# A score row's negated maximum is scaled on ScalarE instead of VectorE

## The chip, the cores and the metric

The kernel runs on one core of a Trainium2 chip. A core has five engines with a queue of instructions each: TensorE (PE in the profile; its weight loads are PEld), VectorE (DVE), ScalarE (ACT), GpSimd (POOL) and SyncE (SP), which here issues the DMAs. An engine takes its instructions in the order of its queue; engines wait for each other through semaphores. The metric is the time on the device in microseconds, lower is better.

## The reference

One layer of an encoder is applied to two groups ("prompt" and "sample") of 1024 tokens with 1024 channels. What matters here are its two attention branches, which read the same normalised input:

```python
qa = rms_norm(qa.reshape(B, S, HQ_A, HEAD_DIM), qn_a)
...
s = jnp.einsum('bqgrd,bkgd->bgrqk', qblk, k).astype(jnp.float32) * scale
p = jax.nn.softmax(s, axis=-1).astype(v.dtype)
return jnp.einsum('bgrqk,bkgd->bqgrd', p, v)
...
p = jax.nn.softmax(s, axis=-1)
pd = (p[:, :, 0] - lam * p[:, :, 1]).astype(v.dtype)
```

Branch A has 8 query heads on 2 key heads of 64 dimensions. Branch B has 4 heads with two softmax maps each, of which the second is subtracted with a learned weight. Queries are normalised by their root mean square before the scores are taken. Around the branches stand one wide input projection, gates with a sigmoid or SiLU, two branch projections, an output projection and a residual add.

## The kernel before

Tokens lie in tiles of 128 rows. Each projection splits its float32 operands into a rounded high part and a low part and adds three products; weights come from memory in four pieces, are rounded on ScalarE (L195), and their low part is taken on GpSimd (L197). The projections of queries, keys and values are L574 (128x256), those of the gates L764 (128x512). TensorE transposes the normalised rows (L637), and ScalarE and VectorE write the two parts of the transposed queries and keys (L639, L640).

A **score unit** (softmax_unit) is one tile of 128 queries against all 1024 keys for one head or map: 256 of them in all, 128 per branch. Four matmuls (L798, L799) fill a PSUM tile s of 1024 columns, of which there are two in turn. VectorE takes the negated maximum of each row into the one-column tile m (L800). The query's inverse root mean square, rs, was not multiplied into the query; it is multiplied into m (L801) and given to the exponential as its scale (L802), so that ScalarE computes exp(rs * s + rs * (-max)) and the row sum in one instruction. m comes from a pool of six buffers, the result p from one of four.

VectorE then transposes p in blocks of 32x32 (L843; in branch B it first subtracts the second map, L842), four DMAs lay the blocks out for TensorE (L852), and a **value unit** multiplies with the values (L866 in branch A, L883 in branch B). The score units of the next query tiles run ahead of these value units.

The code emits attention steps and projection steps interleaved by weights (weave), with a higher priority for attention. A scheduler then sets the order of every engine's queue from a simulated timeline, so that a change of one instruction can move others on all queues. Projections that are ready fill TensorE between score and value units.

Of the kernel before, what the change touches and what calls it, by code (L numbers as in the profile page):

```python
# [14 lines left out]
AF = mybir.ActivationFunctionType  # L15
ALU = mybir.AluOpType
# [73 lines left out]
def kernel(ctx: ExitStack, tc: tile.TileContext, t: dict):  # L90
    nc = tc.nc
# [17 lines left out]
    def nm(s):  # L109
        uid[0] += 1  # L110
        return f"{s}_{uid[0]}"

    def sbank():
        return ps_s.tile([P, 1024], F32, tag="s", name=nm("s"))
# [677 lines left out]
    def softmax_unit(q, sw, k, pt, su, rs):  # L792

        m = tiny.tile([P, 1], F32, tag="m", name=nm("m"))
        s = sbank()
        for n in range(2):
            sl = slice(n * 512, (n + 1) * 512)
            nc.tensor.matmul(s[:, sl], q, k[:, sl], start=True, stop=False)  # L798
            nc.tensor.matmul(s[:, sl], sw, k[:, sl], start=False, stop=True)  # L799
        nc.vector.tensor_reduce(out=m, in_=s, axis=AX.X, op=ALU.max, negate=True)  # L800
        nc.vector.tensor_tensor(out=m, in0=m, in1=rs, op=ALU.mult)  # L801
        nc.scalar.activation(  # L802
            pt.rearrange("p (j c a) -> p j c a", j=4, c=8), s.rearrange("p (c a j) -> p j c a", c=8, j=4),
            AF.Exp, bias=m, scale=rs, accum_out=su,
        )

    def scores(u, i):

        pairs = "h" not in u
        t, m = (i % 2, i // 2) if pairs else (i // 2, i % 2)  # L810
        qt = u["pr"] * 2 + t
        if "sw" not in u:
            u["sw"] = swapped(u)
        pt = ptile()
        if pairs:
            su = u["su"][:, m, qt : qt + 1]
        else:
            su = u["su"][:, qt : qt + 1] if m == 0 else tiny.tile([P, 1], F32, tag="su", name=nm("su"))
        softmax_unit(u["q"][m][:, qt * P : (qt + 1) * P], u["sw"][:, m, t * P : (t + 1) * P], u["k"][m], pt, su, u["rs"][m][:, qt])
        if pairs:  # L820
            u[m, t] = [pt]
            return m, t
        if m == 0:
            u[t] = [pt]
        else:
            f = tiny.tile([P, 1], F32, tag="r", name=nm("r"))
            nc.vector.reciprocal(f, su)
            nc.gpsimd.tensor_scalar(
                out=f, in0=f, scalar1=u["su"][:, qt : qt + 1], scalar2=nlam, op0=ALU.mult, op1=ALU.mult
            )  # L830
            u[t] += [pt, f]
        return (0, t) if m else None
# [559 lines left out]
```

## Time and profile before

| | us |
|---|---|
| timed runs, median of 3 | 1882.31 |
| timed runs, lowest and highest | 1879.48, 1884.93 |
| profiled execution, its span from first to last instruction | 1880.0 |
| median less span | 2.3 |
| TensorE's granted clock, mean share of full speed | 0.995 |

The profiled execution is known by its span; what lies around the span is taken as the 2.3 us to the median. In the profile, a group's line has the line of the kernel, the engine, the operation, output and inputs by name, shapes and count, then the busy time in us, the mean of one in ns, and the engine's idle time before the group with what ended it. In the list of waits, a line has who waited, for whom, the sum in us, how often, and the longest. The windows' lines have start and end, and then the busy time of TensorE, of its weight loads, of VectorE, ScalarE and GpSimd.

### The profile page before, as it was taken

Reading aid. Unit: us, or ns where it says so; the run is one execution under the profiler, and the core shown is the slowest. Engines: PE = TensorE matmul, PEld = TensorE weight load, DVE = VectorE, ACT = ScalarE, POOL = GpSimd, SP = SyncE. Lnnn points to the kernel's source line nnn. Section 1 sums busy time; section 2 is a strip of 40 time slices with the busy share of each in tenths; the row PEclk is TensorE's granted clock in tenths of the full one; section 3 lists DMA queues with packets and bytes.
Section 4 is the critical chain, followed back from the end, with each engine's and each line's share of the span. In section 5 each row is a group of like instructions: output and inputs, shape, how many; then the busy total and the mean of one; then the engine's idle time right before and its main releaser. Section 6 shows DMA issues by size and latency. Waiting matters only on the chain.

```text
span 1880.0 us, 29891 instructions
## 1 busy us (share of the span) xinstructions
PE 1836.5 (98%) x10398; PEld 1550.6 (82%) x10398; DVE 1222.3 (65%) x2016; ACT 780.1 (41%) x1544; POOL 607.1 (32%) x888
## 2 busy tenths in 40 slices
PE   6999999999999999999999999999999999999999
PEld 3798877888899977888889888888888898888887
DVE  5777766454777777347466687666357766663795
ACT  4544434344554444313223445344345545442241
POOL 1243311433454451221233333014354635222100
PEclk8999999999999999999999999999999999999999
DMA  9135776555444567754631567666524343675442
GB/s 324 57 94 160 208 198 178 146 168 163 111 127 113 162 188 219 244 152 140 206 131 52 156 177 204 189 186 188 158 68 141 106 129 103 176 247 173 128 127 92
DMA packets 283895, 295.46 MB, mean 157 GB/s; under 512 B 41952, under 2 KB 236640, under 8 KB 283744
## 3 DMA queue, kind: packets, MB, share of 16 engines
q1 hardware_dynamic: 283744, 293.54, 53.1%
q8 instruction: 83, 1.36, 0.3%
q14 instruction: 68, 0.56, 0.1%
HBM read 133.98 MB, written 42.01 MB: 94 GB/s over the span
## 4 chain that ended last, share of the span: by engine, by line
PE 68%; DMA 4%; issue 3%; DVE 3%; SPq 3%; POOL 2%; ACT 1%; ACTq 0%; DVEq 0%; POOLq 0%
PE f L764 15%; PE f L574 15%; PE f L1038 7%; PE a L883 5%; PE s L798 4%; PE s L799 4%; PE a L866 4%; PE s L1038 3%; PE f L1073 3%; PE s L1073 2%; PE f L1145 2%; SPq L852 1%; DMA q<-p 1%; DMA st<-in_w_in_dram 1%; PE s L1145 1%
## 5 line engine op out<-in xcount | busy, mean ns | idle before, releaser
L764 PE MATMUL f<-u,w 128*128 128x512 f32 x2232 | 565.1, 395 | 0.8 <-POOL w L197 0.4
L574 PE MATMUL f<-w,u 128*128 128x256 f32 x3456 | 478.6, 287 | 0.9 <-POOL w L197 0.4
L764 PEld LDWEIGHTS f<-u,w 128*128 128x128 f32 x2232 | 409.8, 188 | 82.6 <-POOL w L197 1.1
L574 PEld LDWEIGHTS f<-w,u 128*128 128x128 f32 x3456 | 452.3, 193 | 22.3 <-issue 3.5
L800 DVE TENSOR_REDUCE m<-s 128x1 f32<-128x1024 f32 x256 | 309.6, 1218 | 98.8 <-PE s L799 97.4
L197 POOL TENSOR_TENSOR w<-st,w 128x512 fp32r<-128x512 f32 x160 | 213.2, 1350 | 357.9 <-ACT w L195 342.1
L843 DVE STREAM_TRANSPOSE p<-p 128x1024 f32<-128x1024 f32 x192 | 237.7, 1243 | 87.9 <-ACT p L802 73.5
L802 ACT ACTIVATE p<-s,m,u 128x1024 f32<-128x1024 f32 x128 | 153.9, 1204 | 160.0 <-issue 57.8
L802 ACT ACTIVATE p<-s,m,rsB 128x1024 f32<-128x1024 f32 x128 | 154.0, 1204 | 118.7 <-DVE m L801 97.1
L799 PE MATMUL s<-u,sw 128*128 128x512 f32 x512 | 201.1, 397 | 0.0
L195 ACT ACTIVATE w<-st 128x512 fp32r<-128x512 f32 x184 | 108.2, 626 | 112.4 <-DMA st<-in_w_in_dram 97.5
L1038 PE MATMUL f<-u,w 128*128 128x512 f32 x552 | 131.0, 392 | 0.0
L883 PE MATMUL a<-q,u 128*128 128x256 f32 x512 | 126.5, 380 | 4.0 <-DMA q<-p 3.7
L597 POOL TENSOR_TENSOR rsB<-ss,nhalf 128x4 f32<-128x4 f32 x64 | 68.1, 1064 | 184.7 <-DVE ss L596 160.6
L866 PE MATMUL a<-q,u 128*64 128x256 f32 x1024 | 117.7, 382 | 3.6 <-DMA q<-p 2.9
L1038 PEld LDWEIGHTS f<-u,w 128*128 128x128 f32 x552 | 103.0, 188 | 21.1
L798 PE MATMUL s<-u 128*128 128x512 f32 x256 | 107.9, 425 | 2.7 <-ACT p L802 2.7
L799 PEld LDWEIGHTS s<-u,sw 128*128 128x128 f32 x512 | 96.5, 189 | 16.4
L640 DVE TENSOR_TENSOR u<-f,u 64x256 fp32r<-64x256 f32 (+1 forms) x198 | 81.3, 411 | 42.9 <-ACT u L639 37.5
L883 PEld LDWEIGHTS a<-q,u 128*128 128x128 f32 x512 | 93.5, 190 | 18.8 <-issue 3.4
L772 ACT ACTIVATE ev<-f 128x512 f32<-128x512 f32 x93 | 55.3, 595 | 128.5 <-PE f L764 72.5
L866 PEld LDWEIGHTS a<-q,u 128*64 128x64 f32 x1024 | 73.8, 137 | 40.3 <-issue 7.2
(221 smaller groups left out, 2174.6 us busy)
## 6 DMA issues: line engine op xcount, KB each, us to landing
q<-p SPq DMA_DIRECT2D x768, 128.0 KB, 2.6
st<-in_w_in_dram SPq DMA_DIRECT2D x132, 256.0 KB, 3.3
zd<-ev SPq DMA_DIRECT2D x96, 256.0 KB, 2.7
sw<-u SPq DMA_DIRECT2D x256, 64.0 KB, 2.0
u<-in_w_ada_dram SPq DMA_DIRECT2D x8, 1024.0 KB, 11.7
oo<-zd SPq DMA_DIRECT2D x64, 128.0 KB, 2.4
od<-oo SPq DMA_DIRECT2D x64, 128.0 KB, 2.4
st<-in_w_in_dram SPq DMA_DIRECT2D x64, 128.0 KB, 2.7
```

The source lines that it names most:

```text
L195: hi = nc.scalar.activation(wh, st, AF.Copy)
L197: lo = e.tensor_tensor(out=wl, in0=st, in1=wh.bitcast(F32), op=ALU.subtract)
L574: ins = nc.tensor.matmul(ps, lt[c][:, sl], w[:, c, wi, :], start=(k == 0), stop=(k == 23))
L764: ins = nc.tensor.matmul(ps, w[:, c, wi, e * P : (e + 1) * P], rt[c], start=(k == 0), stop=(k == 23),)
L798: nc.tensor.matmul(s[:, sl], q, k[:, sl], start=True, stop=False)
L799: nc.tensor.matmul(s[:, sl], sw, k[:, sl], start=False, stop=True)
L800: nc.vector.tensor_reduce(out=m, in_=s, axis=AX.X, op=ALU.max, negate=True)
L802: nc.scalar.activation(pt.rearrange("p (j c a) -> p j c a", j=4, c=8), s.rearrange("p (c a j) -> p j c a", c=8, j=4), AF.Exp, bias=m, scal ...
L843: nc.vector.transpose(pt, pt)
L866: lambda k=k, m=m: nc.tensor.matmul(acc[(LO, HI)[m]], u["v"][:, k], pT[m][:, k], start=(k == 0), stop=(k == 7))
L883: nc.tensor.matmul(acc, u["v"][:, k], pT[:, k], start=(k == 0), stop=(k == 7))
L1038: nc.tensor.matmul(ps, w[:, c, wi, d * P : (d + 1) * P], o[:, oi, :], start=(k == 0), stop=(k == 11))
```

## The change

The multiplication of m by rs leaves VectorE's queue. ScalarE does it as a copy of one column with rs as its scale, ahead of the exponential that reads m.

```diff
         nc.vector.tensor_reduce(out=m, in_=s, axis=AX.X, op=ALU.max, negate=True)
-        nc.vector.tensor_tensor(out=m, in0=m, in1=rs, op=ALU.mult)
+        nc.scalar.activation(m, m, AF.Copy, scale=rs)
         nc.scalar.activation(
```

The scheduler then orders all queues anew. Three places show it. The numbers in names are those of the tiles; equal names are the same tile in both kernels.

VectorE's queue before, where the second group's branch A begins its second half (near 1160 us in the trace), for the score tiles s_11509 and s_11546:

```order
L800 TENSOR_REDUCE m_11508<-s_11509 128x1
L800 TENSOR_REDUCE m_11545<-s_11546 128x1
L801 TENSOR_TENSOR m_11508<-m_11508,u_9478 128x1
L801 TENSOR_TENSOR m_11545<-m_11545,u_9478 128x1
L774 SCALAR_TENSOR_TENSOR ev_11719<-ev_11719,f_11616 128x512
L843 STREAM_TRANSPOSE p_11507<-p_11507 128x1024
```

The first multiply stands behind the second reduce. VectorE's queue after, for the same two units:

```order
L800 TENSOR_REDUCE m_11508<-s_11509 128x1
L843 STREAM_TRANSPOSE p_11492<-p_11492 128x1024
L843 STREAM_TRANSPOSE p_11507<-p_11507 128x1024
L774 SCALAR_TENSOR_TENSOR ev_11529<-ev_11529,f_11397 128x512
L872 TENSOR_TENSOR oo_11407<-a_11409,oo_11407 128x4x2x32
L800 TENSOR_REDUCE m_11545<-s_11546 128x1
```

The multiplies are gone, and the second reduce has moved behind two transposes.

TensorE's queue before, behind the score tile s_11788 in the same stretch:

```order
L799 MATMUL s_11788<-u_9477,sw_11593 128x512
L764 MATMUL f_11750<-u_9123,w_11733 128x512
L764 MATMUL f_11750<-u_9121,w_11733 128x512 x2
L764 MATMUL f_11750<-u_9123,w_11733 128x512
L764 MATMUL f_11750<-u_9121,w_11733 128x512 x2
L764 MATMUL f_11750<-u_9123,w_11733 128x512
```

In all, 33 matmuls of L764 and L574 stand there before the next score tile, s_11882. TensorE's queue after, at the same tile:

```order
L799 MATMUL s_11788<-u_9477,sw_11593 128x512
L574 MATMUL f_11703<-w_11685,u_9122 128x256
L574 MATMUL f_11703<-w_11685,u_9120 128x256 x2
L574 MATMUL f_11703<-w_11685,u_9122 128x256
L798 MATMUL s_11882<-u_9477,u_10432 128x512
L799 MATMUL s_11882<-u_9477,sw_11593 128x512
L798 MATMUL s_11882<-u_9477,u_10432 128x512
L799 MATMUL s_11882<-u_9477,sw_11593 128x512
L798 MATMUL s_11901<-u_9477,u_10433 128x512
```

Four matmuls of L574 are left between the first two score tiles; s_11901 and s_11932 follow s_11882 with nothing between, then a value unit, then s_11969 and s_12061.

ScalarE's queue before, for three of these score tiles:

```order
L802 ACTIVATE p_11786,suA_138<-s_11788,m_11787,u_9478 128x1024
L772 ACTIVATE ev_11846<-f_11750 128x512
L802 ACTIVATE p_11880,suA_138<-s_11882,m_11881,u_9478 128x1024
L749 ACTIVATE u_11702<-f_11870 128x256
L802 ACTIVATE p_11899,suA_138<-s_11901,m_11900,u_9478 128x1024
```

ScalarE's queue after, from the exponential of s_11788 to the roundings of weights that come behind that of s_11932:

```order
L802 ACTIVATE p_11786,suA_138<-s_11788,m_11787,u_9478 128x1024
L801 ACTIVATE m_11881<-m_11881,u_9478 128x1
L772 ACTIVATE ev_11719<-f_11616 128x512
L802 ACTIVATE p_11880,suA_138<-s_11882,m_11881,u_9478 128x1024
L801 ACTIVATE m_11900<-m_11900,u_9478 128x1
L802 ACTIVATE p_11899,suA_138<-s_11901,m_11900,u_9478 128x1024
L801 ACTIVATE m_11931<-m_11931,u_9478 128x1
L802 ACTIVATE p_11930,suA_138<-s_11932,m_11931,u_9478 128x1024
L195 ACTIVATE w_11685<-st_11694 128x2x256
L195 ACTIVATE w_11685<-st_11698 128x2x256
L195 ACTIVATE w_11733<-st_11734 128x2x256
```

The copies (L801) are new. A tanh (L772) now stands between the copy of m_11881 and its exponential, and pieces of the weights w_11685 and w_11733, which were rounded further ahead before, come behind the exponential of s_11932.

## The prediction

> **What bounds the kernel now.** I read the page's head first, then what TensorE waited for.
>
> ```profile
> span 1880.0 us, 29891 instructions
> PE 1836.5 (98%) x10398; PEld 1550.6 (82%) x10398; DVE 1222.3 (65%) x2016; ACT 780.1 (41%) x1544; POOL 607.1 (32%) x888
> ```
>
> TensorE is busy in 98% of the span, VectorE in 65%, ScalarE in 41%. The change moves work between two engines that have room, so it can touch the end only where TensorE stands still: 1880.0 - 1836.5 = 43.5 us. The windows of 47 us place that idle time.
>
> ```profile
> 0.00:47.00 47.00, 29.47 (x154) 18.08 (x155) 25.59 (x46) 20.65 (x36) 8.87 (x13) 0.85 0.90 324
> 47.00:94.00 47.00, 42.42 (x260) 36.78 (x259) 37.48 (x111) 24.46 (x67) 13.51 (x15) 0.96 0.18 57
> ```
>
> The first number behind the length is TensorE's busy time: 17.5 + 4.6 = 22.1 us of the idle time lie in the first two windows, where no score row exists yet. The rest, 21.4 us, is all that this profile shows to be won. TensorE's waits name its parts.
>
> ```profile
> PE s L798 <- ACT p L802: 4.2, 6, 1.2
> PE a L883 <- DMA q<-p: 3.7, 4, 1.5
> PE f L637 <- POOL row L626: 3.4, 2, 3.2
> PE a L866 <- DMA q<-p: 2.9, 4, 1.3
> PE a L866 <- issue: 0.8, 1, 0.8
> PE a L883 <- issue: 0.3, 1, 0.3
> ```
>
> Two of these hang on the chain that the change edits. A score unit (L798, L799) waits until the exponential (L802) has emptied one of two PSUM buffers: 4.2 us. A value unit (L866, L883) waits for the transposed exponentials to land: 3.7 + 2.9 + 0.8 + 0.3 = 7.7 us. So at most 11.9 us hang on the length of the chain reduce, multiply, exponential, transpose, DMA.
>
> **The multiplication itself.** These groups, with shapes kept apart, carry the prices.
>
> ```profile
> L800 DVE TENSOR_REDUCE m<-s 128x1 f32<-128x1024 f32 x256 | 309.6, 1218 | 98.8 <-PE s L799 97.4
> L801 DVE TENSOR_TENSOR m<-m,u 128x1 f32<-128x1 f32 x128 | 28.2, 226 | 2.7
> L801 DVE TENSOR_TENSOR m<-m,rsB 128x1 f32<-128x1 f32 x128 | 26.6, 215 | 1.9
> L802 ACT ACTIVATE p<-s,m,rsB 128x1024 f32<-128x1024 f32 x128 | 154.0, 1204 | 118.7 <-DVE m L801 97.1 <-issue 11.7 <-DMA q<-p 3.3
> L384 ACT ACTIVATE cT<-cT 128x16 f32<-128x16 f32 x1 | 0.2, 216 | 0.0
> L487 ACT ACTIVATE lam<-lam 128x2 f32<-128x2 f32 x1 | 0.2, 203 | 1.0 <-DVE lam L486 1.0
> L639 ACT ACTIVATE u<-f 64x256 fp32r<-64x256 f32 x182 | 68.3, 375 | 71.2 <-DVE u L640 47.7 <-PE f L637 21.9
> ```
>
> Removed from VectorE: 128 x 226 + 128 x 215 ns = 28.2 + 26.6 = 54.8 us. Added to ScalarE: 256 one-column copies. No row shows one; the nearest are activations on 2 and 16 columns, 203 and 216 ns, and a copy of 256 columns at 375 ns stands above. I take 0.21 us, from the nearest: 256 x 0.21 = 54 us (41 at the 0.159 of VectorE's median multiply, below, and 96 at 0.375 are the ends). ScalarE goes from 780 to some 834 us, 44% of the span, VectorE to 1167. Neither becomes the bound. The multiply's own line gives shortest, median and longest, in ns, which the means hide:
>
> ```profile
> L801 DVE TENSOR_TENSOR m<-m,u x128: 116/159/1260, 130.4 to 1337.5; 128x1 f32<-128x1 f32 x128
> L801 DVE TENSOR_TENSOR m<-m,rsB x128: 118/159/1308, 458.3 to 1682.0; 128x1 f32<-128x1 f32 x128
> ```
>
> The copy issues no DMA and sits at the place in ScalarE's queue where the exponential waited already, so what is queued behind it waited before as well.
>
> [...] The trace has 0.20 to 0.22 us for such small activations, and that is what I use.
>
> **What it does to the chain.** In the trace of before, the multiply often stands behind other VectorE work. The order of instructions has something between reduce and multiply in 176 of 256 units. A stretch where TensorE waits shows what this is worth.
>
> ```profile
> 1161.38 0.50 PE L798 MATMUL s<-u,u 128*128 128x512 f32 x1
> 1162.18 0.40 PE L799 MATMUL s<-u,sw 128*128 128x512 f32 x1
> 1162.41 0.39 PE L798 MATMUL s<-u,u 128*128 128x512 f32 x1
> 1162.61 2.35 DVE L800 TENSOR_REDUCE m<-s 128x1 f32<-128x1024 f32 x2 [0.69 <-PE s L799]
> 1163.32 0.52 PE L574 MATMUL f<-w,u 128*128 128x256 f32 x3
> 1164.88 0.28 DVE L801 TENSOR_TENSOR m<-m,u 128x1 f32<-128x1 f32 x2
> 1165.26 0.60 ACT L772 ACTIVATE ev<-f 128x512 f32<-128x512 f32 x1 [6.38 <-PE f L764]
> 1165.75 1.20 ACT L802 ACTIVATE p<-s,m,u 128x1024 f32<-128x1024 f32 x1
> 1166.94 1.21 ACT L802 ACTIVATE p<-s,m,u 128x1024 f32<-128x1024 f32 x1
> 1167.08 1.25 DVE L843 STREAM_TRANSPOSE p<-p 128x1024 f32<-128x1024 f32 x1 [0.49 <-ACT p L802]
> 1167.10 0.19 PEld L798 LDWEIGHTS s<-u,u 128*128 128x128 f32 x1 [0.29 <-ACT p L802]
> 1168.28 0.19 PEld L798 LDWEIGHTS s<-u,u 128*128 128x128 f32 x1 [0.43 <-ACT p L802]
> ```
>
> The first unit hands TensorE over at 1162.41; its first reduce is done near 1163.8, but its multiply comes only behind the second reduce, at 1164.88, then a tanh (L772) goes first, and the buffer is free again at 1167.0. TensorE takes it at 1167.10: 4.7 us after the hand-over, with 0.29 us waited, and 0.43 us at the next unit. With the multiply on ScalarE the chain at its shortest is 0.20 to the reduce + 1.22 + 0.21 + 1.20 and some 0.3 for three hand-overs (one is 1167.08 - 1166.95 = 0.13), an estimate of **3.1 us**. So the edit gives time back at such spots, and it costs 0.05 us (0.21 - 0.16) where nothing stood between.
>
> **What the new order does.** The scheduler puts the instructions of all queues in a new order, and this weighs more than the edit. I take the work that TensorE has between the end of one score unit and the unit that reuses its buffer, at these prices.
>
> ```profile
> 332.49 3.60 PE a L866 x32
> 370.20 2.87 PE f L574 x24
> 801.98 24.48 PE f L1038 x108
> ```
>
> That is 3.60 us for a value unit (16 in the order, each issued twice), 0.12 us for a 256-column matmul, 0.227 us for a 512-column one and 4 x 0.227 = 0.91 us for a score unit. Before, six places have under 4.5 us, the least 4.30: as many as the six waits above, 0.7 us each, so the chain there took about 5.1 us. After, there are twelve such places from 3.22 to 4.41, and one cluster far below.
>
> In the cluster (s_11788 to s_12061, near 1160 us) eight score units and two value units stand almost side by side. Zero is the hand-over of s_11788. s_11901 needs its buffer after 4 x 0.12 + 0.91 = 1.39 us; the chain takes 3.1, **a wait of 1.7 us**. s_11932 needs the buffer of s_11882, whose reduce ends at 0.20 + 2 x 1.22 = 2.7; copy and hand-overs until 3.2, the tanh that now stands between copy and exponential 0.6, exponential 1.2: free at 5.1. TensorE is there at 3.1 + 0.91 = 4.0, **a wait of 1.1 us**. Behind the cluster L574 needs the last pieces of w_11685, and their rounding is queued on ScalarE behind the exponential of s_11932.
>
> ```profile
> L195 ACT ACTIVATE w<-st 128x512 fp32r<-128x512 f32 x184 | 108.2, 626 | 112.4 <-DMA st<-in_w_in_dram 97.5 <-DMA st<-in_w_out_dram 9.7 <-PE f L1073 2.8
> L197 POOL TENSOR_TENSOR w<-st,w 128x512 fp32r<-128x512 f32 x160 | 213.2, 1350 | 357.9 <-ACT w L195 342.1 <-DMA st<-in_w_in_dram 11.0 <-DMA q<-p 4.5
> L843 DVE STREAM_TRANSPOSE p<-p 128x1024 f32<-128x1024 f32 x192 | 237.7, 1243 | 87.9 <-ACT p L802 73.5 <-DMA q<-p 6.5 <-DMA sw<-u 1.7
> ```
>
> VectorE alternates reduces and transposes (1.22 + 1.24 us a unit), so that exponential ends near 10.3; L195 0.63 and L197 1.35 bring the first missing piece to 12.3. TensorE, after value unit and two scores, is there at 6.0 + 3.6 + 1.8 = 11.4: **0.8 us**. The cluster costs 3.6 us; the least is 2.8 (weights in time), the most 7 (each of the three remaining weight pieces 0.6 to 1.35 us late).
>
> The twelve other places: with a chain of 4.3, the middle between 3.1 and 5.1 rounded up for the copies behind other ScalarE work, the shortfalls add up to 2.8 us (4.3 - 3.22 = 1.1 the largest); with 3.1 nothing, with 5.1 some 12. I take 2.8. For the value units, the work between the last score and the first value matmul was 10.2 us at least and under 12.0 in ten places; after, it is 8.7 in the cluster, whose own waits fill it up, 8.9 at a_1738 and under 12.0 in three more. So I keep half of the 7.7 us and add 2.0 for a_1738 (none to 3).
>
> **Sum.** Gone: 4.2 + 3.9 = 8.1 us. Come: 3.6 + 2.8 + 2.0 = 8.4 us. Against the profiled span of 1880.0 this is +0.3, so 1880.3; the median of the timed runs, 1882.3, lies 2.3 above the span, which gives 1882.6. **I predict 1883 us**: no change that can be told. A measurement of this kernel tells about 0.3%, 5.6 us, from no change: below 1876.7 is faster, above 1888.0 slower.
>
> **Rivals.**
>
> Shorter chain, faster: all 11.9 us of chain waits go and the tight places cost nothing beyond 2.8 in the cluster. Where no such cluster cost shows either, 1882.3 - 11.9 = 1870; with it, 1873. For it: the multiply stood behind other work in 176 units. Against it: twice as many tight places as before. Chance 0.22.
>
> Exponential held on ScalarE, slower: in 68 of 256 units the new order has other ScalarE work between copy and exponential, roundings that wait for a DMA and tanhs that wait for TensorE among it. If the chain at tight places stays at 5.1 us, they cost 12.2, the cluster 7 and a_1738 2; less the 8.1 gone, 1882.3 + 13 = 1895. It decides from a chain of about 4.8 us on, where the shortfalls at the twelve places reach 8.6. Chance 0.23.
>
> Weights late, slower: the new order leaves L574 or L764 waiting for L197 at more than one place. Each late piece is 1.35 us; five to six make 8 us, 1890. The waits on L197 in before were 0.4 us, which speaks against it. Chance 0.05.
>
> The copy is charged to every unit: 256 x 0.05 us = 13 us, 1895, if no unit had cover. TensorE waited for the exponential 6 times, so this would be 0.3 us. It is within the 0.23 above. [...]
>
> Edit without effect on the end, my forecast: 1883, within 1877 to 1888. Chance 0.50.
>
> **Range.** From the first rival with part of the cluster, 1872, to the second, 1895; about 0.1 lies outside on either side. Faster 0.22, same 0.50, slower 0.23 + 0.05 = 0.28.
>
> **What would show it.** Right: VectorE's busy time near 1167 and ScalarE's near 834 us; the copy at 0.20 to 0.22 us; in TensorE's waits for the exponential 3 to 7 us, with 2 to 3 near 1160 us; waits on q DMAs below 7.7. Wrong: a copy of 0.37 us; waits at L798 above 10 us (second rival) or below 2 (first); waits on L197 of several us; or a change in TensorE's idle time at places where no score row is near.

## The result and the profile after

The changed kernel takes **1888.24 us** (median of 5 runs, 1887.49 to 1896.32) where the kernel before takes 1880.20 beside it (median of 5, 1879.48 to 1884.93; the 1882.31 named earlier is the median of the first three of them). The ratio is 1.0047, with a 95% interval of 1.0028 to 1.0066. The forecast was 1883, with no change as the likeliest case; the time lies inside the range of 1872 to 1895, but 5 us above the forecast, and with 0.47% it is on the slower side of the 0.3% that the prediction took for what a measurement can tell. Against the 1880.20 beside it the loss is 8.0 us, where the prediction's sum had 0.3.

The head of the page of the changed kernel, to be set beside 1880.0, 1836.5, 1222.3 and 780.1 us of before:

```profile
span 1885.7 us, 30067 instructions
PE 1840.3 (98%) x10398; PEld 1551.7 (82%) x10398; DVE 1178.2 (62%) x1760; ACT 848.3 (45%) x1800; POOL 605.5 (32%) x888
```

The span is 5.7 us longer. TensorE's idle time (span less busy time) goes from 43.5 to 45.4 us, 1.9 more. Its busy time grows by 3.8 us, although it runs the same 10398 matmuls. So most of what this one execution lost is not waiting. It is matmuls that took longer, and the clock will show why; other executions will show that this does not hold for the change as a whole.

TensorE's waits in the changed kernel (line, what it waited for: us in total, times, longest). The rows that the argument uses are:

```profile
PE s L798 <- ACT p L802: 7.9, 4, 2.9
PE f L637 <- POOL row L626: 2.1, 3, 0.9
PE f L574 <- ACT w L195: 1.9, 1, 1.9
PE a L866 <- DMA oo<-zd: 1.7, 1, 1.7
PE a L883 <- DMA q<-p: 1.2, 2, 1.1
PE f L574 <- POOL w L197: 1.0, 2, 0.5
PE a L883 <- DMA zd<-ev: 0.8, 1, 0.8
PE a L866 <- DMA q<-p: 0.8, 1, 0.8
```

The waits for exponentials have grown from 4.2 to 7.9 us and are fewer and longer: four instead of six, the longest 2.9 instead of 1.2. The waits for q<-p have shrunk from 6.6 to 2.0 us.

The windows of the second group's attention stage (start and end, length, then TensorE busy with its count of matmuls, weight loads, VectorE, ScalarE, GpSimd, the granted TensorE clock, DMA share, GB/s). First the kernel before, then the changed one:

```profile
1173.00:1185.00 12.00, 12.00 (x70) 8.88 (x69) 5.41 (x7) 4.39 (x8) 1.29 (x1) 1.00 0.77 217
...
1125.00:1235.00 110.00, 108.94 (x657) 88.58 (x655) 74.49 (x100) 46.21 (x85) 19.75 (x23) 1.00 0.71 194
```

```profile
1173.00:1185.00 12.00, 7.10 (x32) 3.91 (x32) 9.27 (x9) 6.73 (x13) 0.00 (x0) 0.72 0.75 208
...
1125.00:1235.00 110.00, 105.10 (x622) 82.45 (x621) 69.83 (x74) 53.67 (x107) 19.66 (x22) 0.97 0.70 193
```

Between 1173 and 1185 us TensorE runs 32 matmuls instead of 70, at a clock of 0.72. Over 110 us it is 35 matmuls behind. This is the cluster of the prediction. The timeline of the changed kernel shows how it goes (start, duration, engine, line, out<-in; in brackets the idle time before it and what ended it):

```profile
1169.44 0.59 SPq L777 DMA_DIRECT2D zd<-ev  x1
...
1172.09 0.60 ACT L772 ACTIVATE ev<-f 128x512 f32<-128x512 f32 x1 [2.08 <-DMA zd<-ev]
...
1172.72 0.69 DVE L774 SCALAR_TENSOR_TENSOR ev<-ev,f 128x512 f32<-128x512 f32 x1 [1.12 <-ACT ev L772]
...
1172.98 0.39 PE L799 MATMUL s<-u,sw 128*128 128x512 f32 x1
1173.32 2.35 DVE L800 TENSOR_REDUCE m<-s 128x1 f32<-128x1024 f32 x2
...
1174.58 0.29 ACT L801 ACTIVATE m<-m,u 128x1 f32<-128x1 f32 x1 [1.89 <-DVE m L800]
1174.90 1.20 ACT L802 ACTIVATE p<-s,m,u 128x1024 f32<-128x1024 f32 x1
...
1176.10 0.28 ACT L801 ACTIVATE m<-m,u 128x1 f32<-128x1 f32 x1
...
1176.25 0.50 PE L798 MATMUL s<-u,u 128*128 128x512 f32 x1 [2.88 <-ACT p L802]
...
1177.65 0.60 ACT L772 ACTIVATE ev<-f 128x512 f32<-128x512 f32 x1 [1.26 <-DMA zd<-ev]
1178.14 1.20 ACT L802 ACTIVATE p<-s,m,u 128x1024 f32<-128x1024 f32 x1
...
1179.48 0.79 PE L798 MATMUL s<-u,u 128*128 128x512 f32 x1 [2.02 <-ACT p L802]
1180.07 0.63 PE L799 MATMUL s<-u,sw 128*128 128x512 f32 x1
```

Read it backwards from TensorE. The score unit at 1176.25 waited 2.88 us for an exponential that started at 1174.90, because its reduce started only at 1173.32, because VectorE first had the product L774 in its queue. That waited for the tanh L772 at 1172.09, and this for the transfer zd<-ev, which empties the one buffer of the gate pieces. The next tanh, at 1177.65, stands between a copy and its exponential, and TensorE waits again, 2.02 us. Behind that the score matmuls take 0.63 us instead of 0.39; the granted clock was 0.52 from 1177 to 1184 us.

### The profile page after: what moved, and what is told of

It reads as the page before. It is cut to its first block, busy times and chain, and to the rows that moved or that the text cites. A ratio compares the mean times of both kernels' runs of the same rounds, so it can differ in the third digit from the quotient of the medians.

```text
span 1885.7 us, 30067 instructions
## 1 busy us (share of the span) xinstructions
PE 1840.3 (98%) x10398; PEld 1551.7 (82%) x10398; DVE 1178.2 (62%) x1760; ACT 848.3 (45%) x1800; POOL 605.5 (32%) x888
## 3 DMA queue, kind: packets, MB, share of 16 engines
q8 instruction: 83, 1.36, 0.3%
## 4 chain that ended last, share of the span: by engine, by line
PE 82%; DMA 4%; DVE 4%; issue 3%; ACT 3%; POOL 2%; SPq 2%; ACTq 0%; POOLq 0%; DVEq 0%
PE f L764 21%; PE f L574 19%; PE f L1038 7%; PE a L866 6%; PE s L798 5%; PE s L799 5%; PE a L883 4%; PE s L1038 3%; PE f L1073 3%; PE s L1073 2%; PE f L1145 2%; DMA st<-in_w_in_dram 2%; SPq L852 1%; PE s L1145 1%; PE f L637 1%
## 5 line engine op out<-in xcount | busy, mean ns | idle before, releaser
L764 PE MATMUL f<-u,w 128*128 128x512 f32 x2232 | 573.2, 397 | 0.4 <-POOL w L197 0.3
L764 PEld LDWEIGHTS f<-u,w 128*128 128x128 f32 x2232 | 412.4, 189 | 85.0 <-issue 1.8
L574 PE MATMUL f<-w,u 128*128 128x256 f32 x3456 | 475.2, 286 | 3.7 <-ACT w L195 1.9
L574 PEld LDWEIGHTS f<-w,u 128*128 128x128 f32 x3456 | 449.6, 192 | 25.4 <-issue 3.1
L197 POOL TENSOR_TENSOR w<-st,w 128x512 fp32r<-128x512 f32 x160 | 213.0, 1348 | 355.1 <-ACT w L195 320.3
L802 ACT ACTIVATE p<-s,m,u 128x1024 f32<-128x1024 f32 x128 | 154.2, 1205 | 8.2 <-DMA q<-p 4.8
L195 ACT ACTIVATE w<-st 128x512 fp32r<-128x512 f32 x184 | 108.3, 626 | 106.2 <-DMA st<-in_w_in_dram 93.2
L802 ACT ACTIVATE p<-s,m,rsB 128x1024 f32<-128x1024 f32 x128 | 154.2, 1204 | 3.7 <-ACT m L801 0.2
L1038 PE MATMUL f<-u,w 128*128 128x512 f32 x552 | 131.0, 392 | 0.0
L883 PE MATMUL a<-q,u 128*128 128x256 f32 x512 | 124.3, 380 | 2.2 <-DMA q<-p 1.2
L866 PE MATMUL a<-q,u 128*64 128x256 f32 x1024 | 119.0, 385 | 2.4 <-DMA oo<-zd 1.7
L883 PEld LDWEIGHTS a<-q,u 128*128 128x128 f32 x512 | 94.4, 190 | 17.2 <-DMA zd<-ev 2.1
L866 PEld LDWEIGHTS a<-q,u 128*64 128x64 f32 x1024 | 73.9, 138 | 42.1 <-issue 8.4
L798 PE MATMUL s<-u,u 128*128 128x512 f32 x256 | 103.1, 404 | 4.9 <-ACT p L802 4.9
```

Source lines behind the costliest of these rows:

```text
L195: hi = nc.scalar.activation(wh, st, AF.Copy)
L197: lo = e.tensor_tensor(out=wl, in0=st, in1=wh.bitcast(F32), op=ALU.subtract)
L574: ins = nc.tensor.matmul(ps, lt[c][:, sl], w[:, c, wi, :], start=(k == 0), stop=(k == 23))
L764: ins = nc.tensor.matmul(ps, w[:, c, wi, e * P : (e + 1) * P], rt[c], start=(k == 0), stop=(k == 23),)
L802: nc.scalar.activation(pt.rearrange("p (j c a) -> p j c a", j=4, c=8), s.rearrange("p (c a j) -> p j c a", c=8, j=4), AF.Exp, bias=m, scal ...
L866: lambda k=k, m=m: nc.tensor.matmul(acc[(LO, HI)[m]], u["v"][:, k], pT[m][:, k], start=(k == 0), stop=(k == 7))
```

## Experiments

The theory to be tested is the prediction's: the new order sets the time, not the copy. Its rival is that the copy sets it, by its own time or its place on ScalarE. The change does two things at once: it moves 256 multiplications, and it leads the scheduler to another order of everything. To part them, the kernels below build the program once for its order, edit that order, and build it again with each queue tied to it, instruction behind instruction:

```python
def pin(tc, order):
    ...
    for names in order.values():
        for a, b in zip(names, names[1:]):
            tc.add_manual_dep(traced[b], a, dep)
```

The added lines move the later line numbers: L801, L802, L866 and L883 are L804, L805, L870 and L887 in the runs below (the multiply of e1 and e3 is L802). Where an expectation speaks of matmul 6300 or 6600, this is the number of a matmul in the trace's TensorE records in order of their start, and its "1117 to 1176 us" count from the first matmul, some 7.6 us after the start of the span. Each ratio is against the kernel before on the same chip. A profile is of one execution, and not always a typical one: those of e1 (1901.87 us) and e6 (1891.8) are the slowest of their kernels, those of e5 (1892.58) and e10 (1884.51) the fastest.

**e1: the new order without the copy.** The order of the changed kernel; the multiplication on VectorE, right behind its reduce.

```diff
-        nc.scalar.activation(m, m, AF.Copy, scale=rs)
+        mul = nc.vector.tensor_tensor(out=m, in0=m, in1=rs, op=ALU.mult)
```

> Every queue keeps the order of the changed kernel, but the multiply is back on VectorE, right behind its reduce. Theory A (the new order of the queues costs the time, not the copy): as the changed kernel, 1.0035 to 1.005 of before, some 1887 us, with TensorE waits of 2 us near 692 us and 4 to 5 us near 1176 us. Theory B (the copies on ScalarE cost the time): back at before, 1.000 plus or minus 0.001, 1880 us.

Measured: 1891.19 us, ratio 1.0055 (1.0034 to 1.0077). The loss is there without the copy. But e1 changes more than the order: its multiply stands right behind its reduce, and that alone will cost 0.25% in e3. The clean comparison is the next one, e2 against the changed kernel: both have the copy, and only the order differs. In e1's profile the two units of the cluster wait 2.50 and 1.99 us, as expected, the one near 692 us only 1.14.

**e2: the copy without the new order.** The order of before; the copy on ScalarE, right ahead of its exponential.

```diff
-        nc.vector.tensor_tensor(out=m, in0=m, in1=rs, op=ALU.mult)
+        mul = nc.scalar.activation(m, m, AF.Copy, scale=rs)
```

> Every queue keeps the order of before, but the multiply is the copy on ScalarE, right ahead of its exponential. Theory A: as before, 0.999 to 1.001 of it, 1879 to 1882 us; 256 copies at 0.29 us make 75 us more ScalarE work, and TensorE's wait for exponentials stays near 4 us. Theory B: as the changed kernel, 1.004 or more, 1888 us.

Measured: 1881.79 us, ratio 1.0002 (0.9989 to 1.0015). The copy itself costs nothing that can be told; the interval leaves room for 2.8 us at most. The changed kernel, with the same copy and the new order, has 1.0028 to 1.0066, so the order costs the time. Tying the queues costs nothing that can be told either, since e2's are tied. One of the copy's two rows in e2, among the groups with shapes kept apart:

```profile
L804 ACT ACTIVATE m<-m,u 128x1 f32<-128x1 f32 x128 | 37.0, 289 | 108.6 <-DVE m L800 104.7 <-POOL row L626 3.2
```

These 128 copies take 37 us, but ScalarE stood idle 109 us in front of them, most of it waiting for reduces. TensorE waited 4.1 us for exponentials there, where before had 4.2.

**e3: the order of before, the multiply right behind its reduce on VectorE.** A shorter chain, without the copy.

> The order of before, all on VectorE, but each multiply stands right behind its reduce. It measures what the shorter chain alone is worth. Theory A, with TensorE as the bound: 0.998 to 1.000 of before, 1877 to 1880 us, TensorE's wait for exponentials 4.2 us going to 1 to 3. If chain length were what matters everywhere: 0.994 or less, 1870 us.

Measured: 1886.78 us, ratio 1.0025 (1.0014 to 1.0035): a miss. TensorE's waits for exponentials did fall to 2.2 us, but those of the value units for q<-p rose:

```profile
PE a L870 <- DMA q<-p: 4.7, 4, 1.6
PE f L637 <- POOL row L626: 3.6, 1, 3.6
...
PE a L887 <- DMA q<-p: 2.6, 2, 1.7
...
PE s L798 <- ACT p L805: 2.2, 2, 1.5
```

VectorE was busy for 1242.9 us instead of 1222.3. A shorter chain at each unit does not make this kernel faster; which of these waits made it slower was not tried.

**e4: the new order, two places mended.** Near 690 us the exponential goes ahead of a rounding (L195) that waited for its weights between copy and exponential; in the cluster the tanh goes behind its exponential and two products L774 behind their reduces.

```diff
 ScalarE's queue in the cluster
 L801 copy m_11881
-L772 tanh ev_11719
 L802 exponential p_11880
+L772 tanh ev_11719
```

> The changed kernel with its order, save at two places: near 692 us two exponentials go directly behind their copies, ahead of a weight rounding that waits for a DMA; near 1176 us a tanh goes behind the exponential that it preceded, and two gate multiplies on VectorE behind the reduces. Theory A with these two places as the cause, their waits (2.2 and 4.9 us) and the half-speed clock behind each: 0.9995 to 1.002 of before, 1879 to 1884 us, no stretch of granted clock 0.5 near 696 and 1178 us. If the cost is spread over the whole order or lies in the copies: 1.0035 or more, 1887 us.

Measured: 1889.26 us, ratio 1.0037 (1.0023 to 1.0051). TensorE's waits for exponentials fell from 7.9 to 2.5 us, and no gain can be told: the value unit behind the cluster now waited 1.9 us for q<-p, and the stretch from 1173 to 1185 us still ran at a clock of 0.72.

**e5 to e8: where in the order the loss lies.** The two orders agree on every queue in the middle of the first group's output projection, and at some points around the cluster, so that pieces of the one can be put into the other; the copy is on ScalarE in all four.

```diff
+        order[key] = a[:lo] + b[lo:hi] + a[hi:]
```

e5 is the order of before with the stretch around the cluster from the new one:

> All queues in the order of before, the copy on ScalarE ahead of its exponential, except one stretch of the second group's attention stage (from 1133 to 1233 us in the profiles of both kernels), in which every queue has the order of the changed kernel. Theory S (one stretch): at the same tile the profiled executions of e1, e4 and of the changed kernel fall back by 5 to 6.5 us between 1117 and 1176 us, and e2 and e3 don't, so this stretch carries the loss: 1887 to 1888 us, ratio 1.0025 to 1.0035. Rival D (spread out): the loss is the sum of many small waits over the whole order, and those profiles fell on one place by chance: this stretch is 100 of 1880 us and costs under 1 us, ratio 1.000 to 1.001.

e6 is its counterpart:

> The counterpart: all queues in the order of the changed kernel, but the stretch from 1133 to about 1270 us in that of before. Theory S: 1882 to 1884 us, ratio 1.000 to 1.001. Rival D: 1887 to 1889 us, ratio 1.003 to 1.004, since what is spread over the rest of the order stays.

e7 has the new order in the first group alone:

> The order of the changed kernel up to the middle of the first group's output projection (about 815 us), that of before from there; the copy on ScalarE. By the profiles of before and after the first group loses 1.4 us to the output projection, which the second group takes back by 1045 us. Theory S: 1881.5 to 1883.5 us, ratio 1.000 to 1.001. Rival D: the loss goes by the share of the orders that are new, some 45% of it: 1885 us, ratio 1.0015 to 1.002.

e8 has it in the second alone:

> The counterpart: the order of before up to the middle of the first group's output projection, that of the changed kernel from there. Theory S: 1887 to 1889 us, ratio 1.003 to 1.004, since the stretch at 1133 to 1233 us lies in it. Rival D: 1885 to 1886 us, ratio 1.0015 to 1.0025.

Measured: e5 1895.80 us, ratio 1.0084 (1.0052 to 1.0117); e6 1886.45, 1.0023 (1.0012 to 1.0035); e7 1884.08, 1.0017 (1.0004 to 1.0029); e8 1886.75, 1.0029 (1.0015 to 1.0042). The two groups add up: 0.0017 + 0.0029 = 0.0046, against 0.0047 for the whole change. By these ratios a third of the loss lies in the first group, which the one-place theory excluded; but e7's interval begins at 1.0004, so this share is not certain. Taking the new order out of the stretch alone gives back 0.0047 - 0.0023 = 0.0024 or 4.5 us, more than a spread-out loss would, though the intervals of the two overlap. And both of these joined orders have a seam with a price of its own. e5 waits at 1131.86 us, and e6 at 1273.41, where neither parent does:

```profile
1131.86 0.80 PE L798 MATMUL s<-u,u 128*128 128x512 f32 x1 [3.88 <-ACT p L805]
```

```profile
1273.41 0.80 PE L798 MATMUL s<-u,u 128*128 128x512 f32 x1 [3.17 <-ACT p L805]
```

So e5, which came out worse than either theory foresaw, says little about the stretch, and e6 may give back less than the stretch costs. The traces allow a fairer comparison. Up to the 4600th, the 6300th and the 7200th matmul (near 813, 1125 and 1275 us in before) all the kernels have run the same matmuls, by the names of their tiles without the numbers. So the time between these points is the time for the same work:

| matmuls of the profiled execution | order of before there | new order there |
|---|---|---|
| 1 to 4600 | 800.0 to 805.8 us (before, e2, e3, e5, e8, e10) | 804.1 to 812.9 us (after, e1, e4, e6, e7, e9, e11, e12) |
| 4600 to 6300 | 310.5 to 314.0 | 310.5 to 316.1 |
| 6300 to 7200 | 149.1 to 151.0 (before, e2, e3, e7) | 153.8 to 157.7 (after, e1, e4, e8, e9, e11, e12) |
| 7200 to the last | 601.4 to 604.7 | 600.3 to 604.4 |

Between 6300 and 7200 the two orders do not overlap: the means differ by 5.3 us. e5, with its seam, takes 164.1 us there, and e6 155.1, but its last hundred matmuls, behind the seam, take 20.9 where the order of before has 14.8 to 16.0; up to them e6 is as fast as before. In the first group the means differ by 4.4 us and the ranges overlap. So, as far as these executions show, the stretch of theory S carries more than half of the loss, and the rest is most likely in the first group.

**e9 and e10: the gate pieces' transfers.** In the new order SyncE issues zd<-ev behind long runs of q<-p. SyncE's queue in the changed kernel and, below it, in the kernel before (the duration of a row spans all its transfers):

```profile
1143.09 10.36 SPq L852 DMA_DIRECT2D q<-p  x15
1153.50 0.60 SPq L777 DMA_DIRECT2D zd<-ev  x1
...
1159.16 10.23 SPq L852 DMA_DIRECT2D q<-p  x14
1169.44 0.59 SPq L777 DMA_DIRECT2D zd<-ev  x1
...
1182.27 1.07 SPq L222 DMA_DIRECT2D st<-in_w_in_dram  x2
```

```profile
1141.24 2.86 SPq L852 DMA_DIRECT2D q<-p  x4
1144.20 0.54 SPq L777 DMA_DIRECT2D zd<-ev  x1
...
1152.83 5.16 SPq L852 DMA_DIRECT2D q<-p  x8
1158.09 0.54 SPq L777 DMA_DIRECT2D zd<-ev  x1
```

The gate piece that the changed kernel sends at 1169.44 was ready when its L774 ended, at 1157.61 us; it waited 11.8 us behind fourteen other transfers. e9 moves three of these transfers forward in the new order, e10 moves two of them back in the order of before.

```diff
 SyncE's queue, e9
 od<-oo
+zd_11532<-ev_11529
 q<-p x14
-zd_11532<-ev_11529
```

> All queues in the order of the changed kernel, but on SyncE's queue three of the gate pieces' transfers zd<-ev (issued at 1153.50, 1169.44 and 1175.08 us in the profile of after) stand 26, 15 and 4 transfers earlier. Theory Q (the loss at 1117 to 1176 us comes from these transfers standing behind runs of 14 and 15 q<-p transfers, so that tanhs wait on ScalarE with the exponentials behind them): ScalarE's waits for zd<-ev at 1150 to 1200 us go from 4.5 to under 2 us, the stretch from matmul 6300 to 6600 takes 52 to 55 us (58.6 in after, 51.9 in before), and the time is 1883 to 1886 us, ratio 1.001 to 1.0025. Rival P (the q<-p transfers themselves are late there, and anything put ahead of them makes them later): the stretch stays at 57 us or more, 1887 to 1890 us, ratio 1.003 to 1.005.

> The reverse: all queues in the order of before, the copy on ScalarE ahead of its exponential, but two transfers zd<-ev (issued at 1144.20 and 1158.09 us in the profile of before) stand 13 and 12 transfers later on SyncE's queue, so that the tanhs that wait for them start some 4 us later. Theory Q: the stretch from matmul 6300 to 6600 takes 55 to 60 us (51.9 in before, 52.8 in e2), 1885 to 1888 us, ratio 1.002 to 1.0035. Rival P: the tanhs have cover, and the q<-p transfers come earlier: 52 to 53 us, 1881 to 1883 us, ratio 0.9995 to 1.001.

Measured: e9 1889.15 us, ratio 1.0040 (1.0024 to 1.0056); e10 1888.79 us, ratio 1.0046 (1.0031 to 1.0061). The two disagree. e10 shows that such a wait can cost as much as the whole change: the tanhs waited 6.73 and 7.53 us, TensorE 4.51 us at one score unit, and the matmuls from 6300 to 7200 took 156.3 us.

```profile
1167.90 0.80 PE L798 MATMUL s<-u,u 128*128 128x512 f32 x1 [4.51 <-ACT p L805]
```

But e9 removes the tanhs' waits of the changed kernel (4.5 us between 1150 and 1200 us, now 0.4), and the time does not fall by anything that can be told. Its two score units in the cluster still wait:

```profile
1175.87 0.50 PE L798 MATMUL s<-u,u 128*128 128x512 f32 x1 [1.66 <-ACT p L805]
1178.27 0.79 PE L798 MATMUL s<-u,u 128*128 128x512 f32 x1 [1.21 <-ACT p L805]
```

These are the two waits that the prediction had worked out from the chain alone, 1.7 and 1.1 us. What the late transfers add in the changed kernel's execution, 1.2 and 0.8 us, is gone in e9's, but that does not show in the time. From matmul 6300 to 6600 e9 took 57.4 us, as rival P expected, and e10 59.8, as theory Q did. Up to matmul 6600 the two orders have not run the same matmuls, though; up to 7200 e9 took 154.4 us and the changed kernel 154.9.

**e11 and e12: TensorE's missing work.** From 1169 to 1177 us before has some forty projection matmuls between its score units; the changed kernel has twelve. Twelve more of the same projection stand behind the cluster, since the second half of their weights (the two transfers st<-in_w_in at 1182.27 above) is late too. e11 moves these transfers, their roundings and the twelve matmuls forward; e12 adds e9.

```diff
 TensorE's queue, e11
 L798 s_11882
+L574 f_11703 x6
 L798 s_11901
+L574 f_11703 x6
 L798 s_11932
 L866 a_11812
...
-L574 f_11703 x12
```

> All queues in the order of the changed kernel, but the second half of the weights w_11685 (two transfers st<-in_w_in, issued at 1182.27 us in the profile of after, where before has them at about 1140 us) stands 42 transfers earlier on SyncE's queue, its two roundings behind the exponential at 1161.48 us on ScalarE, and the twelve projection matmuls that need it six and six ahead of the score tiles that waited 2.88 and 2.02 us. Theory W (in the new order the score tiles stand together because the projection matmuls that before has between them have no weights yet): the twelve matmuls (0.15 us each, 1.8 us) come out of the waits for exponentials, which go from 4.9 to about 3 us, and the half-clock windows behind them from two to one or none: 1884 to 1887 us, ratio 1.0015 to 1.003; the stretch from matmul 6300 to 6600 goes from 58.6 to 54 to 57 us. Rival P (the transposes q<-p or the exponentials are late in any case): the wait moves to the value unit behind, 58 us or more, 1887.5 to 1890 us, ratio 1.0035 to 1.005.

> e11 and e9 together: the weights and the twelve matmuls earlier, and the three transfers zd<-ev too. Theory W: e9's two waits of 1.66 and 1.21 us are covered by 0.9 us of matmuls each, about 1 us is left, with no half-clock window: 1882.5 to 1885.5 us, ratio 1.0005 to 1.0025, the stretch 53 to 55.5 us. Rival P: 57 us or more, 1887 to 1890 us, ratio 1.003 to 1.005.

Measured: e11 1888.23 us, ratio 1.0042 (1.0028 to 1.0056); e12 1888.84 us, ratio 1.0046 (1.0030 to 1.0062). Again no gain can be told. In e11's profile the half clock is gone from the cluster, and TensorE runs 51 matmuls in this window instead of 32 (the cluster's waits also come 3 us later there):

```profile
1173.00:1185.00 12.00, 8.13 (x51) 6.74 (x51) 8.91 (x10) 5.75 (x11) 0.00 (x0) 1.00 0.74 210
```

But the score units still wait 2.50 and 1.36 us. In e12 they wait 0.86 and 1.67, and the value unit behind them waits too:

```profile
1178.42 0.50 PE L798 MATMUL s<-u,u 128*128 128x512 f32 x1 [0.86 <-ACT p L805]
1181.99 0.50 PE L798 MATMUL s<-u,u 128*128 128x512 f32 x1 [1.67 <-ACT p L805]
1184.77 5.22 PE L870 MATMUL a<-q,u 128*64 128x256 f32 x32 [1.58 <-DMA q<-p]
```

From matmul 6300 to 6600 e11 took 55.8 us, as theory W expected, and e12 57.0, but both times are those of rival P. The matmuls that TensorE ran from 1125 to 1235 us, by which order the kernel has there:

| order from 1125 to 1235 us | matmuls | ratio of the whole kernel |
|---|---|---|
| of before: before, e2, e3, e6, e7 | 657, 655, 650, 663, 652 | 1, 1.0002, 1.0025, 1.0023, 1.0017 |
| new: after, e1, e5, e8 | 622, 623, 578, 615 | 1.0047, 1.0055, 1.0084, 1.0029 |
| new, mended: e4, e9, e11, e12 | 621, 626, 628, 609 | 1.0037, 1.0040, 1.0042, 1.0046 |
| of before, spoilt: e10 | 616 | 1.0046 |

Each count is of one execution and of a fixed time, in which a kernel that is behind does other work (e1 is 11 us behind by then); but the two orders do not overlap, 650 to 663 against 578 to 628, and by the same work they did not either. No repair of one place brought the number back.

## Why the prediction was off

**The cause was named rightly.** The prediction said that the new order weighs more than the edit. e2 and the changed kernel show it: the copy in the old order costs nothing that can be told, the copy in the new order 0.47%. The price of the order was not named rightly: the sum had 0.3 us for it.

**The copy was mis-sized, without harm.** It was taken at 0.21 us; the line's row has 0.29 us:

```profile
L801 ACT ACTIVATE m<-m,u x128: 278/294/297, 129.8 to 1343.4; 128x1 f32<-128x1 f32 x128
```

The 256 copies take 74.6 us instead of 54, and ScalarE comes to 848 instead of 834 us (VectorE to 1178 instead of 1167). As e2 shows, the longer copy made no difference that can be told: ScalarE stood idle in front of the copies, 109 us at 128 of them. This also settles the rival that charged the copy to every unit: it had 13 us, and e2's interval ends at 2.8.

**What goes.** 8.1 us were to go, 4.2 + 3.9. The value units' waits for q<-p, with the issue rows beside them, fell from 7.7 to 2.0 us, 5.7 against the 3.9 expected. The six short waits for exponentials went too: outside the places below 7.9 - 2.88 - 2.02 - 2.19 = 0.8 us are left.

**What comes.** The twelve tight places were to cost 2.8 us and cost at most this 0.8. The chain did become shorter: from the last score matmul to the end of the exponential the median of the 256 units is 4.36 us in before, 3.88 in e2 and 3.42 in the changed kernel, where the prediction took 4.3 for the twelve places. That is the mechanism of its first rival, which came true without making the kernel faster. The wait at a_1738 was to be 2.0 us and was 0.77, within the 2.0 above. The cluster was to cost 3.6, 1.7 + 1.1 at the two score units and 0.8 for weights, and cost 2.88 + 2.02 = 4.9 at the score units alone. What this term had wrong is the zero of its clock: it took reduce and tanh to start as soon as TensorE handed over, and did not read SyncE's queue, where the transfers that free the tanh's buffer had moved behind runs of fourteen. Without them, in e9, the two waits are 1.66 and 1.21. Most of the loss lies elsewhere, since without these late transfers e9 is not faster by anything that can be told. One place had no term: near 692 us a rounding that waits 2.42 us for its weights came between a copy and its exponential, and TensorE waited 2.19. This is the mechanism of the second rival, exponentials held on ScalarE, at one place instead of everywhere. The late weights of the third rival show at one place too, 1.9 us at L574 behind L195, and the value units have new waits for other transfers, 1.7 + 0.8 us. Together: 4.2 + 5.7 = 9.9 us gone; 4.9 + 2.2 + 0.8 + 1.9 + 2.5 = 12.3 come; with 0.6 more for L197 at L574 and 1.3 less for L626 a balance of 1.7, near the 1.9 us that the idle time grew. (For L197 the prediction read 0.4 us of waits in before; it is 0.4 at L574 and 0.4 more at L764.) That the forecast of +0.3 lies near these 1.9 is in part luck: the wait at 692 us, the late weights and the two other transfers, 6.6 us, had no term, and the tight places and a_1738, 4.8 us, did not come in their size. By the prediction's own signs, the waits for exponentials, 7.9 us, lie above its 3 to 7 and below the 10 of the second rival, and the 4.9 near 1176 us above its 2 to 3.

The wait near 692 us is not the order's alone. The same unit waited 2.19 us in the changed kernel and 2.37 in e6, but 1.14 in e7, 1.20 in e9 and 0.90 in e12, all with the same order there; with the old order a unit at this place waited 1.12 us in before and 2.37 in e2. The rows of the changed kernel, of e7 and of e2:

```profile
694.29 0.50 PE L798 MATMUL s<-u 128*128 128x512 f32 x1 [2.19 <-ACT p L802]
```

```profile
694.57 0.50 PE L798 MATMUL s<-u 128*128 128x512 f32 x1 [1.14 <-ACT p L805]
```

```profile
696.15 0.50 PE L798 MATMUL s<-u 128*128 128x512 f32 x1 [2.37 <-ACT p L805]
```

So how long this unit waits differs from one execution to the next, and that e4 shows no wait there is no proof of its repair.

**What had no term.** TensorE's idle time rose by 1.9 us where the sum had 0.3, a small error. The other 3.8 us are in its busy time, and the sum had nothing for that: it counted waits, and not the half clock that followed some of them. Windows of the changed kernel around the wait at 692 us:

```profile
690.00:696.00 6.00, 3.67 (x27) 1.62 (x26) 2.45 (x6) 3.69 (x7) 3.00 (x3) 1.00 0.48 134
696.00:703.00 7.00, 7.00 (x22) 5.61 (x22) 3.69 (x6) 2.26 (x6) 0.90 (x2) 0.51 0.43 135
703.00:709.00 6.00, 6.00 (x30) 4.99 (x29) 2.95 (x4) 2.38 (x5) 0.34 (x1) 1.00 0.64 176
```

TensorE is busy through the 7 us behind the wait, at 0.51 of its clock, which loses it 7 x 0.49 = 3.4 us; from 1177 to 1184 us, in the cluster, the granted clock was 0.52. This accounts for the profiled execution, and not for the medians. By the clock record, TensorE ran at half its clock behind the first 94 us for 13.7 us in this execution and for 3.4 in before's; but for 10.2 in e2's, which lost nothing, and for 6.8 in e10's and in e12's, which both lost 0.46%. In e11 and e12 TensorE's idle time was 49.5 and 50.0 us at a busy time of 1840, so there the loss shows as waiting.

**What stays open.** The loss is the order's, about 3 us in the first group and 5.5 in the second by e7 and e8, and in the second mostly between 1125 and 1275 us, where the same work takes 5 us longer. Which item of that order makes it is not settled. Three repairs of three different waits (exponential ahead of tanh, transfers, weights with the matmuls that need them) each changed the wait that they were made for. None took the whole loss away: the lowest interval of the four runs begins at 1.0023, and e2's ends at 1.0015. But the changed kernel's own interval is 0.19% to either side and theirs some 0.15%, so that a gain of several us could hide in any one of them. The first group's share was not followed to a place, and a part of the stretch on a single queue was not tried.

## What to carry to other kernels

Where a scheduler sets the order, a small edit is two changes: pin the old order with the new instruction, and the new order with the old one, before a reason is looked for in the instruction. Read the DMA-issuing queue of the new order as closely as the engines' own: here a transfer that frees a single buffer had slipped behind fourteen others, and it went out 11.8 us late. And where an engine is 98% busy, as here, mending the wait that is named may win nothing, as e4, e9, e11 and e12 show. So weigh an order by the time that its bottleneck takes for the same work, between points at which both orders have done the same, and look at more than one execution before a wait is called the order's.

## What the runs showed of the hardware

TensorE's granted clock fell to half behind some waits, in the clock record for 3.4 us (before, from 1003 us on) or 6.8 us (the changed kernel, from 696 and from 1177 us on), and not behind others of the same length. At one and the same place (L637, waiting for GpSimd's L626), before waited 3.21 us and e2 3.15. The windows that hold the wait and the time behind it, of before and then of e2:

```profile
1392.00:1396.00 4.00, 2.10 (x18) 2.10 (x19) 3.83 (x8) 1.08 (x2) 3.84 (x10) 1.00 0.50 131
1396.00:1404.00 8.00, 8.00 (x50) 7.13 (x49) 6.42 (x9) 3.49 (x9) 3.87 (x8) 1.00 0.45 112
```

```profile
1394.00:1398.00 4.00, 3.34 (x18) 3.34 (x19) 3.11 (x6) 2.55 (x6) 3.66 (x10) 0.57 0.39 107
```

Before kept its full clock, 1.00 in both windows, and e2 did not: 0.57 over the 4 us that hold the end of its wait. A longer wait was not the surer one either: the 3.21 us of before were followed by the full clock, the changed kernel's 2.19 us at 692 us by 7 us at 0.51. What decides whether the clock falls behind a wait was not shown.

The one-column copy on ScalarE, whose factor is a column in SBUF, took 0.29 us in the changed kernel and in e2, where activations of 2 and 16 columns with a fixed factor (L487 and L384, one of each in before) took 0.20 and 0.22; what makes the difference was not tried apart.
